# Splitting the first experts' weights on VectorE alone, in a routed encoder block in f32

## The chip, the cores and the metric

The kernel runs on one core of one Trainium2 chip. Its time is the device time of one execution in microseconds (us). Several runs were made; the median and the spread stand below, and one more execution was recorded by the hardware profiler.

## What is computed

One encoder block over 1024 positions of width 1024, in f32. A mixing half comes first (a Fourier group and windowed attention, an output projection, a gated residual). Then a mixture of 16 experts in which each expert chooses its 128 tokens:

```python
def expert_choice_moe(h, w_router, w_gate, w_up, w_down):
    cap = CAPACITY_FACTOR * S // N_EXPERTS          # 2 * 1024 / 16 = 128
    aff = jax.nn.softmax(h @ w_router, axis=-1)     # (S, 16)
    g, idx = lax.top_k(aff.T, cap)                  # each expert's 128 best tokens
    xin = h[idx]
    a, u = xin @ w_gate, xin @ w_up                 # 1024 x 1024 each, per expert
    y = (silu(a) * u) @ w_down * g
    return zeros.at[idx].add(y)
```

Each expert has three weight matrices of 4 MiB, 192 MiB for all sixteen. The change concerns only the second half, and its start above all.

## The kernel before

**Products in three parts.** A product of f32 values is made from three TensorE passes: both operands are split into a high part (the value rounded to TensorE's f32 format) and a low part (what is left), and hi x hi, lo x hi and hi x lo are summed (`mm3`, L71 to L74). `split` (L76 to L78) makes the parts: ScalarE copies the value into the high part (L77), then VectorE, or GpSimd where the caller says so, subtracts (L78). So in the profile L77 is a ScalarE piece of a split, and L78 the subtraction, on whichever engine it runs. `raw` is the tile that a load lands in, `wh` and `wl` are a weight unit's high and low part, `t0h`, `t0l`, `t1h`, `t1l` those of an expert's transposed tokens.

**Units and steps.** The expert weights are cut into 192 units of 1 MiB (256 rows by 1024 columns), four to a matrix, in the order gate 0, up 0, gate 1, down 0, up 1, gate 2, down 1, and so on (L962 to L967). A step is one unit's product, twelve matmuls of 512 columns. `load` (L970) issues a unit's load on SP's queue into one of 13 raw buffers; unit 13 goes into the buffer of unit 0, unit 14 into that of unit 1, so each can be loaded only once the other has been split. `cut_unit` (L989) splits the next unit into one of four pairs of `wh` and `wl`, and asks for the next load. `ahead` (L1140) keeps three units split ahead of the step that is about to run. In the kernel before, units 0 and 1 are split by GpSimd in four pieces each, as soon as they are loaded, while the last sort of the mixing half still runs; of units 6 to 23 the even ones go to GpSimd in two pieces, the odd ones to VectorE whole; all others go to VectorE.

**How the first experts are chosen.** While the last tile of the mixing half (t = 7) is projected, VectorE sorts the affinities of the tiles 0 to 5: steps of elementwise maximum and minimum over 32 x 64 elements (L805 and L806, tiles `sc` and `R`), and the result goes into `best` and `bestT`. L716 and L717 are the residual of the last tile, in two halves; L752 and L763 transpose it and form its affinities. From its affinities `choose` (L1063) finds the tokens of one expert in steps that wait for each other through TensorE; it runs for expert 0, then for expert 1. For the other 14 experts `thresholds` (L1106) sorts once more and counts; its steps are drawn in `product` between the first two experts' products, and its end is `dg` (L1115), a small product with it, a comparison (L1058, L1059), a count on TensorE (L1045, L1047) and `cn` (L1050).

**Gathering.** `gather_a` (L1161) makes eight marks for an expert (`oneh`, L1165: one where a position equals a slot), one per tile, on GpSimd or VectorE. `gather` (L1168) multiplies them with token numbers and gates on TensorE (L1173), VectorE forms the index `idx` (L1175), and GpSimd issues an indirect DMA that fetches the expert's rows from `h2d` into `xe` (L1182). `h2d` is in DRAM; the last tile's rows are written there at L1132. `flip` (L1186) transposes the tokens (L1192) and splits them. In the kernel before GpSimd makes two of the marks of expert 0 and four of those of expert 1, none of experts 2 and 3, and all of the later ones.

**Order.** Every engine works through its instructions in the order of the program. Where the code calls `in_order`, that order is the order in which the code was written, for the engines named; elsewhere a scheduler interleaves. The stretch from the second `choose` to the first product is pinned for TensorE, VectorE and GpSimd among its own instructions, and the experts' loop for all engines; the first instructions of the former can still be moved ahead of older ones. SP's queue is one line of loads and writes: a load that waits for a buffer holds up everything written behind it. The load of unit 11 (`HELD`) is held until the first gather has been issued.

Of the kernel before, what the change touches and what calls it, by code (L numbers as in the profile page):

```python
# [21 lines left out]
NT = 8  # L22
# [14 lines left out]
NSW, RATE0, RATE1, RATE2 = 5, 3.0, 2.0, 1.3  # L37
TK = 3

EARLY, LATER, HELD = (0, 1, 2, 3, 9, 10), (13, 14, 4, 5, 6, 7, 8), 11  # L40


@with_exitstack
def block_kernel(ctx: ExitStack, tc: tile.TileContext, t_in, out):
    nc = tc.nc
    PE, ACT, DVE, POOL, SP = nc.tensor, nc.scalar, nc.vector, nc.gpsimd, nc.sync
# [17 lines left out]
    def pt(name="pt"):  # L64
        return ps.tile([128, 512], F32, name=name, tag="pt", bufs=2)
# [10 lines left out]
    def split(hi, lo, src, eng=None):  # L76
        ACT.activation(hi, src, AF.Copy)  # L77
        return (eng or DVE).tensor_tensor(lo, src, hi.bitcast(F32), op=OP.subtract)  # L78
# [36 lines left out]
    def traced():  # L115
        return len(nc.cur_bb.bb.instructions)
# [10 lines left out]
    def drain(g):  # L127
        for _ in g:
            pass
# [836 lines left out]
    units_ = [(w[e], u) for w, e in groups for u in range(4)]  # L966
    NR = RAW1 + RAW2 + RAW3  # L967
    raws, cut = {}, []

    def load(m=None):  # L970
        if m is None:
            m = next((i for i in range(len(units_)) if i not in raws), None)
            if m is None:
                return
        src, u = units_[m]
        rp = raw3 if m % NR < RAW3 else raw2 if m % NR < RAW3 + RAW2 else raw1
        r = rp.tile([128, 2, D], F32, name="raw", tag="raw")
        if m == HELD:
            with tc.issue_after(after["p"].ins):
                POOL.memset(r[0:1, 0, 0:1], 0.0)  # L980
        v = src.rearrange("(k p) c -> p k c", p=128)[:, 2 * u:2 * u + 2, :]
        if m == len(units_) - 1:
            for k in range(2):
                SP.dma_start(r[:, k], v[:, k])
        else:
            SP.dma_start(r, v)
        raws[m] = r

    def cut_unit(eng=None, parts=1):  # L989
        m = len(cut)  # L990
        if m == len(units_):
            return
        r = raws[m]
        wp = wa if m % 4 in (0, 1) else wk
        h = wp.tile([128, 2, D], F32R, name="wh", bufs=2)
        l = wp.tile([128, 2, D], F32R, name="wl", bufs=2)
        for c in range(0, 2 * D, 2 * D // parts):
            hv, lv, rv = (o.rearrange("p k c -> p (k c)")[:, c:c + 2 * D // parts] for o in (h, l, r))
            split(hv, lv, rv, eng)
        cut.append((h, l))  # L1000
        if m > 1:
            load()

    pa, = banks(ctx, "psM", pa=6)
    for m in EARLY:
        load(m)
    for _ in range(2):
        cut_unit(POOL, 4)
    g2_r = wk.tile([128, D], F32, name="g2_r")
    tri = rt.tile([128, 128], BF, name="tri")  # L1010
    r1 = rt.tile([128, NT, NE], F32, name="r1")
# [29 lines left out]
    def counted(gq, es):  # L1041
        m = gq.shape[1]
        n = gq.shape[2]
        p = pa()
        PE.matmul(p[:, :m * n], tri, gq.rearrange("p a e -> p (a e)"), start=True, stop=False)  # L1045
        for a in range(m - 1):
            PE.matmul(p[:, (a + 1) * n:m * n].rearrange("p (a e) -> p a e", e=n), ones_b,  # L1047
                      gq[:, a:a + 1, :].to_broadcast([128, m - 1 - a, n]), start=False, stop=(a == m - 2))
        c = rt.tile([128, m, n], F32, name=f"cn{n}")
        DVE.scalar_tensor_tensor(c.rearrange("p a e -> p (a e)"), p[:, :m * n], 1.0, gq.rearrange("p a e -> p (a e)"),  # L1050
                                 op0=OP.add, op1=OP.mult)
        return c

    def at_least(th, nt, es):
        n = es.stop - es.start
        gq = rt.tile([128, 2 * nt, n], BF, name=f"gq{n}")
        th = th[:, None, :].to_broadcast([128, nt, n])
        DVE.tensor_tensor(gq[:, :nt], aff[:, :nt, es], th, op=OP.is_gt)  # L1058
        DVE.tensor_tensor(gq[:, nt:], aff[:, :nt, es], th, op=OP.is_equal)  # L1059
        return gq  # L1060


    def choose(e):  # L1063
        p = pt()
        for i in range(2):
            PE.matmul(p[:, i * 128:i * 128 + 128], aff[:, OLD + i, e:e + 1].to_broadcast([128, 128]), ident,
                      start=True, stop=True)
        acc = rt.tile([128, 5], F32, name="acc")
        v6, v7 = aff[:, OLD, e:e + 1], aff[:, OLD + 1, e:e + 1]

        def above(a, val):
            junk = rt.tile([128, 256], BF, name="junk", bufs=2)
            return DVE.scalar_tensor_tensor(junk, p[:, :256], val, ones, op0=OP.is_gt, op1=OP.mult, accum_out=acc[:, a:a + 1])

        above(0, best[:, e:e + 1])
        kept = rt.tile([128, 1], BF, name="kept")
        k0 = DVE.tensor_scalar(kept, acc[:, 0:1], rank0, 127.0, op0=OP.add, op1=OP.is_le)
        with tc.issue_after(k0.ins):
            above(1, v6)
        yield  # L1080
        pn = pa()
        PE.matmul(pn[:, :1], ones_b, kept, start=True, stop=True)
        edge = rt.tile([128, 1], F32, name="edge")
        e0 = DVE.scalar_tensor_tensor(edge, pn[:, :1], rank1, best[:, e:e + 1], op0=OP.is_equal, op1=OP.mult)
        with tc.issue_after(e0.ins):
            above(3, v7)
            for a, val, w, wid in ((2, v6, below, 128), (4, v7, both, 256)):
                junk = rt.tile([128, 256], BF, name="junk", bufs=2)
                DVE.scalar_tensor_tensor(junk[:, :wid], p[:, :wid], val, w, op0=OP.is_equal, op1=OP.mult,
                                         accum_out=acc[:, a:a + 1])  # L1090
        yield
        pe = pa()
        PE.matmul(pe[:, :1], ones[:, 0:128], edge, start=True, stop=True)
        gq = at_least(pe[:, :1], OLD, slice(e, e + 1))
        yield
        c = counted(gq, slice(e, e + 1))
        a, b = c[:, :OLD, 0], c[:, OLD:, 0]
        DVE.tensor_tensor(a, a, b, op=OP.add)
        DVE.scalar_tensor_tensor(pos[:, :OLD, e], a, pn[:, :1], a, op0=OP.is_le, op1=OP.mult)
        for i in range(2):  # L1100
            r = acc[:, 1 + 2 * i:2 + 2 * i]
            DVE.scalar_tensor_tensor(r, r, 1.0, acc[:, 2 + 2 * i:3 + 2 * i], op0=OP.add, op1=OP.add)
            DVE.tensor_tensor(pos[:, OLD + i, e:e + 1], r, pn[:, :1], op=OP.add)
# [36 lines left out]
    def ahead(la):  # L1140
        while len(cut) <= step[0] + la and len(cut) < len(units_):
            m = len(cut)
            if 6 <= m < 24 and m % 2 == 0:
                cut_unit(POOL, 2)
            else:
                cut_unit(None, 2 if m == len(units_) - 1 else 1)

    def product(acc, xh, xl, la=3, halves=False):
        n = step[0]
        u = n % 4  # L1150
        if n:
            drain(itertools.islice(rest, 3))
        ahead(la)
        step[0] += 1
        wh, wl = cut[n]
        for k, hf in ((0, 0), (1, 0), (0, 1), (1, 1)) if halves else ((0, 0), (0, 1), (1, 0), (1, 1)):
            kc = 2 * u + k
            cs_ = slice(hf * 512, hf * 512 + 512)
            mm3(acc[hf], xh[:, kc, :], xl[:, kc, :], wh[:, k, cs_], wl[:, k, cs_], kc == 0, kc == 7)

    def gather_a(e):  # L1161
        shared = (2, 4, 0, 0)[e] if e < 4 else NT
        oneh = wk.tile([128, NT, 128], BF, name="oneh", bufs=1)
        for t in range(NT):
            (POOL if t < shared else DVE).tensor_scalar(oneh[:, t, :], slots, pos[:, t, e:e + 1], None, op0=OP.is_equal)  # L1165
        return oneh
# [19 lines left out]
    def flip(src, e):  # L1186
        h = wk.tile([128, 8, 128], F32R, name=f"t{e % 2}h", bufs=1)
        l = wk.tile([128, 8, 128], F32R, name=f"t{e % 2}l", bufs=1)
        for b in range(2):
            p = pt()  # L1190
            for k in range(4):
                PE.transpose(p[:, k * 128:k * 128 + 128], src[:, (4 * b + k) * 128:(4 * b + k + 1) * 128], ident)  # L1192
            split(h[:, 4 * b:4 * b + 4], l[:, 4 * b:4 * b + 4], p.rearrange("p (a b) -> p a b", b=128))
        return h, l
# [18 lines left out]
    gs = {}  # L1213
    gather(0)
    tp = traced()
    while len(raws) < NR + 2:
        load()
    SP.dma_start(g2_r, md[3:4, :].to_broadcast([128, D]))
    c1 = choose(1)
    next(c1)  # L1220
    next(c1)
    cut_unit(parts=2)
    drain(c1)
    oneh = gather_a(1)
    xh, xl = flip(gs[0][2], 0)
    cut_unit()

    def selection():
# [117 lines left out]
```

## Time and profile before

| | us |
|---|---|
| median of 3 runs | 1079.47 (1076.07 to 1079.58) |
| the profiled execution | 1078.71 |
| its span in the profile | 1076.9 |
| PE busy | 969.0 (90%) |
| DVE busy | 845.9 (79%) |
| ACT busy | 636.9 (59%) |
| POOL busy | 540.3 (50%) |
| chain that ended last, by engine | PE 64%, DVE 15%, issue 6%, ACT 4%, DMA 2%, POOL 2% |

PE is TensorE, PEld its weight loads, DVE VectorE, ACT ScalarE, POOL GpSimd, SP the engine that issues most DMAs. A row of a timeline has the start in us from the span's start, the duration in us, the engine, the line, the operation, the tile written and those read, the shapes and a count; in brackets stand the engine's idle time before it and what ended that. A row of a stage has its length, the busy time of each engine with its number of instructions, the clock granted to TensorE (1.00 is full), the share of time that the 16 DMA engines were busy, and GB/s. A row of waits has who waited for whom, the sum in us, how often, and the longest. The later experts fill the span from about 558 us on; the routing of the first ones lies between about 400 and 558 us.

### The profile page before, as it was taken

What the parts mean: (1) busy time and instruction counts of PE and PEld (TensorE: products, weight loads), DVE (VectorE), ACT (ScalarE), POOL (GpSimd) and SP (SyncE); (2) the same over time, 40 slices, a digit from 0 to 9 for tenths busy, and PEclk for the clock granted to TensorE, in tenths of its full rate; (3) what the DMA queues carried; (4) which work ended last, traced back from release to release, by engine and by line L of the source; (5) the groups of instructions that cost most, each with busy time, mean ns of one, the idle gap of its engine ahead of it and who ended that gap; (6) DMA issues with size and microseconds to landing.
All of it is one profiled execution on the core that took longest, in us unless ns stands there. A gap on an engine that the chain in (4) does not pass through costs nothing.

```text
span 1076.9 us, 13229 instructions
## 1 busy us (share of the span) xinstructions
PE 969.0 (90%) x4681; PEld 756.4 (70%) x4681; DVE 845.9 (79%) x1223; ACT 636.9 (59%) x846; POOL 540.3 (50%) x345
## 2 busy tenths in 40 slices
PE   4797999979999996496769999999999999999996
PEld 3675767747777675374658777877787778777885
DVE  6845884687666959689688898889888988898894
ACT  3353434576455442264437777777777777777782
POOL 2646465132433334355472875587558755772203
PEclk9798999979999999598889999999999999999998
DMA  9765674262312136895689999999999999999922
GB/s 318 246 210 212 220 266 150 82 195 61 111 70 89 65 132 215 326 321 192 229 260 339 410 372 374 369 411 370 373 369 411 371 371 371 411 371 358 376 110 40
DMA packets 95499, 283.97 MB, mean 264 GB/s; under 512 B 7892, under 2 KB 25480, under 8 KB 95304
## 3 DMA queue, kind: packets, MB, share of 16 engines
q1 hardware_dynamic: 90824, 266.34, 66.7%
q0 software_dynamic: 4608, 16.78, 6.1%
q8 instruction: 37, 0.61, 0.2%
q14 instruction: 30, 0.25, 0.1%
HBM read 263.79 MB, written 21.40 MB: 265 GB/s over the span
## 4 chain that ended last, share of the span: by engine, by line
PE 64%; DVE 15%; issue 6%; ACT 4%; DMA 2%; POOL 2%; POOLq 0%; DVEq 0%; ACTq 0%; SPq 0%
PE pa L72 13%; PE pa L73 13%; PE pa L74 13%; PE pu L332 4%; PE pt L1192 2%; ACT wh L77 2%; PE pt L640 2%; PE yp L653 2%; DVE sc L805 2%; DVE wl L78 2%; PE pj L74 2%; PE pj L72 2%; PE pj L73 2%; DVE sc L806 2%; DVE ws L113 2%
## 5 line engine op out<-in xcount | busy, mean ns | idle before, releaser
L78 DVE TENSOR_TENSOR wl<-raw,wh 128x2048 fp32r<-128x2048 f32 (+1 forms) x183 | 418.1, 2309 | 63.5 <-ACT wh L77 62.6
L77 ACT ACTIVATE wh<-raw 128x2048 fp32r<-128x2048 f32 (+2 forms) x209 | 367.8, 1780 | 85.0 <-PE pa L73 81.3
L1165 POOL TENSOR_SCALAR oneh<-tri_f,pos 128x128 bf16<-128x128 f32 x102 | 189.5, 1871 | 4.1 <-PE pa L1047 3.3
L73 PE MATMUL pa<-wh,t1l 128*128 128x512 f32 x384 | 151.8, 395 | 7.8 <-DVE t1l L78 7.8
L72 PE MATMUL pa<-wh,t0h 128*128 128x512 f32 x384 | 155.8, 406 | 0.0
L73 PE MATMUL pa<-wh,t0l 128*128 128x512 f32 x384 | 153.4, 400 | 0.0
L72 PE MATMUL pa<-wh,t1h 128*128 128x512 f32 x384 | 153.1, 399 | 0.0
L74 PE MATMUL pa<-wl,t0h 128*128 128x512 f32 x384 | 152.6, 397 | 0.0
L74 PE MATMUL pa<-wl,t1h 128*128 128x512 f32 x384 | 151.3, 394 | 0.0
L1207 POOL TENSOR_TENSOR ys<-ys,g_r 128x512 f32<-128x512 f32 x30 | 53.5, 1803 | 124.7 <-ACT ys L1206 124.7
L73 PEld LDWEIGHTS pa<-wh,t1l 128*128 128x128 f32 x384 | 72.6, 189 | 24.0 <-DVE t1l L78 8.3
L74 PEld LDWEIGHTS pa<-wl,t0h 128*128 128x128 f32 x384 | 73.6, 192 | 17.0
L72 PEld LDWEIGHTS pa<-wh,t0h 128*128 128x128 f32 x384 | 73.6, 192 | 16.2 <-ACT t0h L77 0.2
L73 PEld LDWEIGHTS pa<-wh,t0l 128*128 128x128 f32 x384 | 73.6, 192 | 16.1 <-DVE t0l L78 0.4
L74 PEld LDWEIGHTS pa<-wl,t1h 128*128 128x128 f32 x384 | 72.6, 189 | 17.0 <-DVE wl L78 0.4
L72 PEld LDWEIGHTS pa<-wh,t1h 128*128 128x128 f32 x384 | 72.4, 189 | 15.9
L1182 POOL DMA_INDIRECT xe<-h2d,idx x16 | 16.9, 1055 | 115.7 <-DVE gt L1179 110.7
L78 POOL TENSOR_TENSOR wl<-raw,wh 128x1024 fp32r<-128x1024 f32 (+1 forms) x26 | 56.7, 2208 | 22.3 <-ACT wh L77 22.2
L78 POOL TENSOR_TENSOR hl<-hf,hh 128x512 fp32r<-128x512 f32 (+1 forms) x20 | 25.5, 1274 | 62.9 <-ACT hh L77 43.6
L1210 POOL DMA_INDIRECT out_dram<-ys,idx x16 | 50.9, 3183 | 10.6 <-DVE ys L1209 6.4
L611 DVE CUSTOM_DVE_ANT_0 sb<-lg,bias,sink 128x384 f32<-128x384 f32 (+1 forms) x64 | 35.0, 579 | 26.7 <-PE lg L609 15.7
L233 ACT ACTIVATE hf<-pt,sh1c,G1c 128x128 f32<-128x128 f32 (+1 forms) x56 | 22.6, 479 | 53.3 <-PE pt L226 36.2
(310 smaller groups left out, 1809.5 us busy)
## 6 DMA issues: line engine op xcount, KB each, us to landing
raw<-in_w_gate_dram SPq DMA_DIRECT2D x64, 1024.0 KB
raw<-in_w_up_dram SPq DMA_DIRECT2D x64, 1024.0 KB
raw<-in_w_down_dram SPq DMA_DIRECT2D x63, 1024.0 KB
raw<-in_w_ada_dram SPq DMA_DIRECT2D x16, 1024.0 KB
raw<-in_w_ada_dram SPq DMA_DIRECT2D x16, 512.0 KB
xt<-in_x_dram SPq DMA_DIRECT2D x8, 512.0 KB
raw<-in_w_out_dram SPq DMA_DIRECT2D x4, 1024.0 KB
raw<-in_x_dram SPq DMA_DIRECT2D x8, 512.0 KB
```

The costliest lines, as they stand in the source:

```text
L72: PE.matmul(o, lh, rh, start=start, stop=False)
L73: PE.matmul(o, ll, rh, start=False, stop=False)
L74: return PE.matmul(o, lh, rl, start=False, stop=stop)
L77: ACT.activation(hi, src, AF.Copy)
L78: return (eng or DVE).tensor_tensor(lo, src, hi.bitcast(F32), op=OP.subtract)
L113: DVE.scalar_tensor_tensor(acc, u[:, j, :], w, acc, op0=OP.mult, op1=OP.add)
L233: ACT.activation(hf[:, a * w:a * w + w], tp[:, a * w:a * w + w], AF.Identity, scale=G1c[:, kc:kc + 1], bias=sh1c[:, kc:kc + 1])
L332: PE.matmul(acc[:, :c1 - c0], lhs, r[kc][:, c0:c1], start=(kc == 0 and l == 0 and r is w_h), stop=(kc == 7 and r is w_l))
L611: DVE.tensor_tensor_reduce(sb[:, :wid], lg[:, :wid], bias[:, kv * 4 + i, j0:j0 + wid], 1.0, sk[:, i:i + 1], op0=OP.add, op1=OP.max, accum_ ...
L1165: (POOL if t < shared else DVE).tensor_scalar(oneh[:, t, :], slots, pos[:, t, e:e + 1], None, op0=OP.is_equal)
L1207: POOL.tensor_tensor(ys[:, cs_], ys[:, cs_], g2_r[:, cs_], op=OP.mult)
L1210: POOL.indirect_dma_start(out=out2, out_offset=bass.IndirectOffsetOnAxis(ap=idx[:, :1], axis=0), in_=ys, in_offset=None, compute_op=OP.add)
```

## The change

Three things are changed. GpSimd splits no expert weights any more: `cut_unit` loses its engine argument, and `ahead` the rule for units 6 to 23. Units 0 and 1 are no longer split at the start of the stage, but later, in two pieces each: unit 0 behind the first gather, unit 1 between the second and the third step of `choose(1)`; units 2 and 3, whole, behind the first flip. Because `load` of units 13 and 14 needs the buffers of units 0 and 1, they are taken out of `LATER`, and every `cut_unit` now asks for a load. And the marks of experts 0 to 3 are all made by VectorE.

```diff
-EARLY, LATER, HELD = (0, 1, 2, 3, 9, 10), (13, 14, 4, 5, 6, 7, 8), 11
+EARLY, LATER, HELD = (0, 1, 2, 3, 9, 10), (4, 5, 6, 7, 8), 11
...
-    def cut_unit(eng=None, parts=1):
+    def cut_unit(parts=1):
...
-            split(hv, lv, rv, eng)
+            split(hv, lv, rv)
         cut.append((h, l))
-        if m > 1:
-            load()
+        load()
...
     for m in EARLY:
         load(m)
-    for _ in range(2):
-        cut_unit(POOL, 4)
...
     def ahead(la):
         while len(cut) <= step[0] + la and len(cut) < len(units_):
             m = len(cut)
-            if 6 <= m < 24 and m % 2 == 0:
-                cut_unit(POOL, 2)
-            else:
-                cut_unit(None, 2 if m == len(units_) - 1 else 1)
+            cut_unit(2 if m == len(units_) - 1 else 1)
...
     def gather_a(e):
-        shared = (2, 4, 0, 0)[e] if e < 4 else NT
+        shared = 0 if e < 4 else NT
...
     gs = {}
     gather(0)
     tp = traced()
-    while len(raws) < NR + 2:
+    while len(raws) < NR:
         load()
     SP.dma_start(g2_r, md[3:4, :].to_broadcast([128, D]))
+    cut_unit(2)
     c1 = choose(1)
     next(c1)
     next(c1)
-    cut_unit(parts=2)
+    cut_unit(2)
     drain(c1)
     oneh = gather_a(1)
     xh, xl = flip(gs[0][2], 0)
+    cut_unit()
     cut_unit()
```

In the rows of the changed kernel below, lines up to L986 are numbered as before; from L1010 on to `ahead` they read three lower (L1016 is L1013), behind it six (L1165 is L1159).

VectorE, at the end of the last sort. Before, from its last merge steps to the second half of the last tile's residual (`raw<-lg,g_r`, then `raw<-raw`):

```order
L806 TENSOR_TENSOR sc<-sc 32x16x4
L805 TENSOR_TENSOR sc<-sc 32x32x2
L806 TENSOR_TENSOR sc<-sc 32x32x2
L805 TENSOR_TENSOR R<-sc 32x64
L806 TENSOR_TENSOR R<-sc 32x64
L857 STREAM_TRANSPOSE best<-R 32x32 x4
L858 COPY bestT<-R 16x128
L1014 CAST tri<-r_4143 128x128
L1033 TENSOR_TENSOR r_4143<-aff,aux 128x96
L716 TENSOR_TENSOR raw<-lg,g_r 128x512
```

And now, from the first half of unit 0's split:

```order
L78 TENSOR_TENSOR wl<-raw,wh 128x1024
L805 TENSOR_TENSOR sc<-sc 32x2x32
L806 TENSOR_TENSOR sc<-sc 32x2x32
L805 TENSOR_TENSOR sc<-sc 32x4x16
L806 TENSOR_TENSOR sc<-sc 32x4x16
L78 TENSOR_TENSOR wl<-raw,wh 128x1024
L805 TENSOR_TENSOR sc<-sc 32x8x8
L806 TENSOR_TENSOR sc<-sc 32x8x8
L1011 CAST tri<-r_4123 128x128
L805 TENSOR_TENSOR sc<-sc 32x16x4
L806 TENSOR_TENSOR sc<-sc 32x16x4
L716 TENSOR_TENSOR raw<-lg,g_r 128x512
```

Unit 0's two halves have come in between the steps, ahead of where the code has them, and the residual has moved from behind the sort and the copies of its result to ahead of its last two pairs of steps.

SP, from the weights that are loaded last before the first gather to the write of the last tile's rows (`h2d`), the difference of the two orders:

```order
-L1022 DMA tok<-in_k_tok_dram 128x16
-L986 DMA raw<-in_w_down_dram 128x2x1024 x2
+L1010 DMA r_4123<-in_k_tri_dram 128x128
+L1013 DMA tri_f<-in_k_tri_dram 128x3x128
+L1019 DMA tok<-in_k_tok_dram 128x16
 L986 DMA raw<-in_w_up_dram 128x2x1024 x4
 L986 DMA raw<-in_w_gate_dram 128x2x1024
-L1132 DMA h2d<-raw 128x1024
-L1133 DMA out_dram<-raw 128x1024
+L1129 DMA h2d<-raw 128x1024
+L1130 DMA out_dram<-raw 128x1024
```

The two loads of `w_down`, units 13 and 14, are gone from ahead of the write; they now stand behind the load of `g_r`, after the first gather.

VectorE, at the end of `thresholds`, among the products of the second expert's turn. Before:

```order
L1115 TENSOR_SCALAR dg<-ident,R 16x16
L78 TENSOR_TENSOR wl<-raw,wh 128x2048
L1058 TENSOR_TENSOR gq_4745<-aff,pt 128x120
L1059 TENSOR_TENSOR gq_4745<-aff,pt 128x120
L1050 SCALAR_TENSOR_TENSOR cn_4785<-pa,gq_4745 128x240
L1125 TENSOR_TENSOR pos<-cn_4785 128x8x15
L1165 TENSOR_SCALAR oneh<-tri_f,pos 128x128 x8
```

And now:

```order
L1112 TENSOR_SCALAR dg<-ident,R 16x16
L78 TENSOR_TENSOR wl<-raw,wh 128x2048
L1055 TENSOR_TENSOR gq_4725<-aff,pt 128x120
L1056 TENSOR_TENSOR gq_4725<-aff,pt 128x120
L78 TENSOR_TENSOR wl<-raw,wh 128x2048
L1047 SCALAR_TENSOR_TENSOR cn_4763<-pa,gq_4725 128x240
L1122 TENSOR_TENSOR pos<-cn_4763 128x8x15
L1159 TENSOR_SCALAR oneh<-tri_f,pos 128x128 x8
```

A second unit's split, which GpSimd had, stands between the comparison and `cn`. In the same way one more split stands on VectorE at every second step of the first two experts.

## The prediction

> **What bounds the kernel now.** I read the chain that ended last in order of time, then the busy time by stage, then who TensorE waited for, then VectorE's and GpSimd's own timelines where it waited. The chain, from the end of routing:
>
> ```profile
> 441.33 8.78 DMA h2d<-raw
> 451.02 5.22 DMA xe<-h2d,idx
> 456.28 1.97 PE pt L1192 x8
> ...
> 558.26 0.87 PE pt L1192 x8
> ...
> 588.25 1.93 ACT wh L77
> ...
> 624.11 1.92 ACT wh L77
> ```
>
> The first gather waits for the last tile's write to h2d. From 558 us on the same row returns every 35.86 us, one expert. The stages (PE, PEld, DVE, ACT, POOL busy, clock, DMA share, GB/s):
>
> ```profile
> 459.00:558.00 99.00, 73.15 (x318) 57.56 (x319) 85.11 (x127) 46.28 (x42) 58.24 (x28) 0.83 0.73 254
> 566.00:1030.00 464.00, 460.15 (x2171) 371.27 (x2170) 403.81 (x282) 349.70 (x260) 281.92 (x139) 1.00 1.01 379
> ```
>
> Later experts are TensorE's: 460.15 of 464 us. In the first stage TensorE has 73 of 99 us, VectorE 85. TensorE's waits from 456 to 600 us:
>
> ```profile
> PE pt L1119 <- DVE dg L1115: 9.5, 1, 9.5
> PE pt L1173 <- DVE oneh L1165: 8.5, 3, 4.3
> PE pa L73 <- DVE t1l L78: 7.8, 1, 7.8
> ```
>
> All three name VectorE: 25.8 us. And VectorE is held up. The short sort steps beside GpSimd's splits (start, duration):
>
> ```profile
> 417.19 1.35 POOL L78 TENSOR_TENSOR wl<-raw,wh 128x512 fp32r<-128x512 f32 x1 [1.33 <-ACT wh L77]
> 417.29 1.32 DVE L805 TENSOR_TENSOR sc<-sc 32x64 f32<-32x64 f32 x1
> ...
> 421.69 0.21 DVE L806 TENSOR_TENSOR sc<-sc 32x64 f32<-32x64 f32 x1
> 421.71 8.69 POOL L78 TENSOR_TENSOR wl<-raw,wh 128x512 fp32r<-128x512 f32 x7 [3.17 <-ACT wh L77]
> 421.94 1.21 DVE L805 TENSOR_TENSOR sc<-sc 32x64 f32<-32x64 f32 x1
> 423.07 1.30 DVE L806 TENSOR_TENSOR sc<-sc 32x64 f32<-32x64 f32 x1
> ...
> 430.41 0.20 DVE L806 TENSOR_TENSOR R<-sc 32x64 f32<-32x64 f32 x1
> ```
>
> A step takes 0.21 us until GpSimd's split starts, then 1.2 to 1.3, which is one GpSimd piece (8.69 / 7 = 1.24), and 0.20 again once GpSimd is done. I read that as exclusion: one step slips in after each piece.
>
> **The change: before the first product.** Removed: the eight quarter splits of units 0 and 1 on GpSimd. Seven steps took 430.41 - 421.94 = 8.5 us; at 0.21 they take 1.5. With the one at 417.29 (1.32 to 0.21) that is 7.0 + 1.1 = 8.1 us back. Added: unit 0's two halves, which the order puts between those steps; a pair cost 2.36 us, below. Moved: the last tile's second half (L716, L717) used to stand behind the sort, and now stands before its last pairs.
>
> ```profile
> 419.54 0.67 DVE L717 TENSOR_TENSOR raw<-raw 128x512 f32<-128x512 f32 x1
> ...
> 432.09 0.69 DVE L716 TENSOR_TENSOR raw<-lg,g_r 128x512 f32<-128x512 f32 x1
> ...
> 447.35 0.22 DVE L1175 TENSOR_SCALAR idx<-pt 128x1 int32<-128x1 f32 x1
> ...
> 449.43 2.36 DVE L78 TENSOR_TENSOR wl<-raw,wh 128x1024 fp32r<-128x1024 f32 x2
> ...
> 453.55 0.90 DVE L1165 TENSOR_SCALAR oneh<-tri_f,pos 128x128 bf16<-128x128 f32 x4
> 458.06 0.69 DVE L78 TENSOR_TENSOR t0l<-pt,t0h 128x512 fp32r<-128x512 f32 x1 [3.62 <-ACT t0h L77]
> ```
>
> New start of L716: L717's end (420.2) less 1.1; plus a shuffle, a merge and three pairs, which took until 421.9, 1.7; two more pairs 0.8; the halves 2.4; a cast, taken as a step, 0.2: 424.2. So what follows from that half comes 7.9 us earlier; the index, with two more marks on VectorE (0.4), at 447.35 - 7.5 = 439.9.
>
> The write to h2d is then issued at 441.33 - 7.9 = 433.4. With its 8.78 us it lands at 442.2. But ahead of it SP used to have seven loads, and now has five:
>
> ```profile
> 423.32 0.40 PE L74 MATMUL lg<-wol,yah 128*128 128x512 f32 x1
> ...
> 425.55 5.26 SPq L986 DMA_DIRECT2D raw<-in_w_down_dram  x2
> 430.90 2.16 SPq L986 DMA_DIRECT2D raw<-in_w_up_dram  x4
> 433.10 0.49 SPq L986 DMA_DIRECT2D raw<-in_w_gate_dram  x1
> ...
> GB/s 318 246 210 212 220 266 150 82 195 61 111 70 89 65 132 215 326 321 192 229 260 339 410 372 374 369 411 370 373 369 411 371 371 371 411 371 358 376 110 40
> ```
>
> The two of w_down (units 13 and 14) waited for GpSimd, and the others behind them on SP. At 411 GB/s, the highest rate of the slices, 1 MiB is 2.55 us, two are 5.1. Five loads from about 423 us, when the last output product (first row) ends, take 12.8 and are through near 437 with a start of about 1 us; the write's half MiB takes 1.3 and lands near 440, together with the index. Bounds: 7.9 us (queue as long as before) to 10.4 (the index alone); I take 10, since the two loads are gone for certain. VectorE must then be ready for the flip at 458.06 - 10 = 448.1: its last marks end at 454.45 - 7.5 + 0.8 (four more marks) = 447.8. This covers the added work with 0.3 us to spare; any more lies on the path. Unit 2's split moves behind the flip (2.28 us); two products (35.86 / 12 = 3 us each) cover it.
>
> **The stage of the first experts.** VectorE's groups between 459 and 558 us, GpSimd's splits, VectorE's sort (tile sc), and marks without GpSimd beside them:
>
> ```profile
> L78 DVE TENSOR_TENSOR wl<-raw,wh 128x2048 fp32r<-128x2048 f32 x12 | 31.1, 2596 | 4.1 <-ACT wh L77 4.1
> L1165 DVE TENSOR_SCALAR oneh<-tri_f,pos 128x128 bf16<-128x128 f32 x16 | 9.5, 670 | 0.0
> ...
> L78 POOL TENSOR_TENSOR wl<-raw,wh 128x1024 fp32r<-128x1024 f32 x18 | 46.7, 2618 | 17.8 <-ACT wh L77 17.7
> ...
> 459.00:558.00 99.00, 31.68 (x46) 0.83 0.73 254
> ...
> 525.88 1.67 DVE L1165 TENSOR_SCALAR oneh<-tri_f,pos 128x128 bf16<-128x128 f32 x8
> 527.46 2.29 DVE L78 TENSOR_TENSOR wl<-raw,wh 128x2048 fp32r<-128x2048 f32 x1
> ```
>
> Before: 31.1 + 9.5 + 31.7 and 12.8 of other work make 85.1. After, with nothing of GpSimd's splits beside it: 12 units, the 9 from GpSimd and unit 2 are 22 x 2.28 = 50.2; sort 46 x 0.21 = 9.7; marks 16 x 0.21 = 3.3; other 12.8: 76.0 us. So ten units cost 22.8 us more, and 31.9 us of being held go away.
>
> VectorE's idle time in the stage is 99 - 85.1 = 13.9 us. Most of it, with 559 us taken in:
>
> ```profile
> DVE cn L1050 <- PE pa L1047: 4.4, 1, 4.4
> DVE wl L78 <- ACT wh L77: 4.1, 1, 4.1
> DVE t1l L78 <- ACT t1h L77: 3.3, 1, 3.3
> DVE idx L1175 <- PE pt L1173: 1.9, 2, 1.6
> ```
>
> The order now puts another unit's split ahead of cn (2.3 of the 4.4) and unit 3's ahead of idx (1.6): at most 10.0 us stay, at least none. I take 7, near the upper end, because ScalarE's ys and hs still stand ahead of the next wh. The stage: 76 + 7 = 83 for 99, a gain of 16 (13 to 23). TensorE needs 73 us or less for it, so VectorE sets its end. The waits of 25.8 us shrink, not vanish.
>
> **The sum.** The profiled execution is 1078.71 us (span 1076.9), 0.8 under the median. 1078.7 - 10 - 16 = **1053 us**; by the bounds 1058 to 1045. The later experts are TensorE's and move as a whole.
>
> **Does DMA let them?** Its share is 1.01 from 566 to 1030, and the two loads now come later. SP's own waits from 560 to 1040 us:
>
> ```profile
> SPq L986 <- DVE wl L78: 354.6, 142, 7.4
> ```
>
> SP waits most of the time for a free buffer, not for the queue, so TensorE's pace sets the loads. An expert's 12 loads take 12 x 2.55 = 30.6 us of its 35.86. The Trainium skill speaks against this in SBUF — State Buffer, Summary: rules for kernel authors: it has transfers from HBM reckoned at about 358 GB/s; an estimate by it is 2.93 us a load and 35.2 an expert without the gathers, so DMA would be the pace and nothing would be gained. The row above, 379 GB/s over 464 us, is over that rate, and the trace decides.
>
> **Rivals.** *DMA is the pace* of the later experts: the end stays, or comes later by the two loads' 5.1 us: 1079 to 1084. For: share 1.01. Against: SP's waits, and 0.73 in the stage to catch up in. *The front stays*: something else keeps the first gather (the write's queue, or VectorE late with the added splits); only 16 us: 1063. For: the cover of 0.3 us. *The idle time grows* with VectorE as the only splitter: the stage gives 7 instead of 16: 1062. For: ScalarE and TensorE are in one loop with VectorE through four weight buffers. *The other side*: the stretch is not GpSimd's doing, and the short steps stay long because of something that remains. Then VectorE gets 22.8 us more in the stage and 2.4 in the sort: 1078.7 + 25 = 1104. It decides once less than 25 of the 8.1 + 31.9 us come back. Against: at 421.71 and 430.41 the stretch begins and ends with GpSimd's run. That the change is not made as told is excluded by the order.
>
> **How the numbers follow.** Forecast (1045 to 1058): 0.71. Front stays: 0.09. Idle grows: 0.08. Better than 1045: 0.04. DMA the pace: 0.04. Other side: 0.04. A measurement here tells about 0.5% (5.4 us) from no change: faster 0.71 + 0.09 + 0.08 + 0.04 = 0.92, same 0.04, slower 0.04. The range takes in the two smaller gains: 1044 to 1066.
>
> **What would show it.** Right: no sort step over 0.7 us after 417 us; the write to h2d issued near 433.4, the gather near 441, the transposes of 558.26 near 532; VectorE busy some 76 of 83 us there, TensorE's waits about half; every expert after that 35.86 us. Wrong: sort steps of over a microsecond with GpSimd idle; a first product no earlier than 455; TensorE waiting for wh with ScalarE waiting for raw (DMA); VectorE idle over 14 us in the stage.

## The result and the profile after

The changed kernel takes 1045.9 us (median of 4 runs, 1044.96 to 1046.96), the kernel before beside it 1078.91 us. The ratio is 0.9693, 95% interval 0.9675 to 0.9712: 33 us faster, where 26 were forecast. The profiled execution took 1045.42 us, with a span of 1043.6 us, 33.3 under that of before.

The two stages of the profile after, in the columns of the prediction's stage rows: from the first flip's low part to the transposes that stood at 558.26 us before, and a stretch of later experts as long as the one shown of before:

```profile
445.44:524.45 79.01, 70.45 (x320) 55.35 (x321) 73.99 (x139) 45.65 (x33) 12.69 (x9) 0.92 0.93 341
532.00:996.00 464.00, 460.15 (x2171) 371.21 (x2170) 403.60 (x282) 349.57 (x260) 283.97 (x139) 1.00 1.01 379
```

Before, the first of these ran from 458.06 to 558.26 us, 100.2 us; now it takes 79.0, and it starts 12.6 us earlier. VectorE is busy for 74.0 of the 79.0 us, TensorE's clock has gone from 0.83 to 0.92. The second row has TensorE's busy time, 460.15 us, and the 379 GB/s of before to the last digit: the later experts run as they did.

The routing before the first product, on VectorE, SP and GpSimd (start, duration), from the sort steps beside unit 0's halves to the first flip:

```profile
419.15 0.21 DVE L806 TENSOR_TENSOR sc<-sc 32x64 f32<-32x64 f32 x1
419.28 1.21 DVE L78 TENSOR_TENSOR wl<-raw,wh 128x1024 fp32r<-128x1024 f32 x1
420.42 0.20 DVE L805 TENSOR_TENSOR sc<-sc 32x64 f32<-32x64 f32 x1
...
422.89 0.67 DVE L716 TENSOR_TENSOR raw<-lg,g_r 128x512 f32<-128x512 f32 x1
...
437.68 0.22 DVE L1169 TENSOR_SCALAR idx<-pt 128x1 int32<-128x1 f32 x1
...
443.88 1.65 DVE L1159 TENSOR_SCALAR oneh<-tri_f,pos 128x128 bf16<-128x128 f32 x8
445.44 1.28 DVE L78 TENSOR_TENSOR t0l<-pt,t0h 128x512 fp32r<-128x512 f32 x2
```

```profile
416.91 0.61 SPq L1019 DMA_DIRECT2D tok<-in_k_tok_dram  x1
417.62 4.37 SPq L986 DMA_DIRECT2D raw<-in_w_up_dram  x4
422.03 0.74 SPq L986 DMA_DIRECT2D raw<-in_w_gate_dram  x1
432.32 0.34 SPq L1129 DMA_DIRECT2D h2d<-raw  x1
```

```profile
438.20 1.20 POOL L1176 DMA_INDIRECT xe<-h2d,idx  x1 [5.91 <-DVE gt L1173]
```

The sort steps take 0.2 us with a split on either side of them. The residual has come from 432.09 to 422.89 us, the index from 447.35 to 437.68, and the gather now follows the index within 0.52 us, where it used to come 3.67 us after it and waited for the write. The five loads no longer wait; SP issues them right behind the token table.

VectorE's groups in the stage of the first experts (busy, mean ns of one), the time of its sort (tile `sc`) there up to the third expert's `hs`, and what VectorE waited for:

```profile
L78 DVE TENSOR_TENSOR wl<-raw,wh 128x2048 fp32r<-128x2048 f32 x22 | 50.3, 2298 | 1.8 <-ACT wh L77 1.8
L1159 DVE TENSOR_SCALAR oneh<-tri_f,pos 128x128 bf16<-128x128 f32 x16 | 3.3, 278 | 0.0
```

```profile
445.44:559.21 113.77, 8.12 (x46) 0.94 0.92 334
```

```profile
DVE wl L78 <- ACT wh L77: 1.8, 1, 1.8
DVE idx L1169 <- PE pt L1167: 0.7, 2, 0.4
```

The 46 sort instructions took 31.68 us and take 8.12, the marks 9.5 and now 3.3; 22 splits take 50.3. TensorE's waits, from 430 to 600 us:

```profile
PE pt L1167 <- DVE oneh L1159: 4.6, 2, 3.6
...
PE pt L1186 <- DVE hs L1268: 2.5, 3, 1.9
...
PE pt L1116 <- DVE dg L1112: 1.4, 1, 1.4
...
PE pa L73 <- DVE t1l L78: 0.9, 1, 0.9
...
PE pa L73 <- DVE t0l L78: 0.8, 1, 0.8
```

The three waits of 25.8 us are now 4.6 + 1.4 + 0.9 = 6.9 (1.0 of them lies ahead of the first flip, outside the stretch that the prediction counted); those for `hs` have grown from 0.3 to 2.5, and one of 0.8 for `t0l` is new. The prediction had the three at half; they are about a quarter.

### The profile page after: what moved, and what is told of

Same layout as the page of the kernel before. It is cut to its first block, busy times and chain, and to the rows that moved or that the text cites. A ratio compares the mean times of both kernels' runs of the same rounds, so it can differ in the third digit from the quotient of the medians.

```text
span 1043.6 us, 13198 instructions
## 1 busy us (share of the span) xinstructions
PE 964.2 (92%) x4681; PEld 752.6 (72%) x4681; DVE 828.4 (79%) x1241; ACT 636.1 (61%) x832; POOL 482.6 (46%) x313
## 4 chain that ended last, share of the span: by engine, by line
PE 64%; DVE 14%; issue 7%; ACT 4%; POOL 3%; DMA 1%; POOLq 0%; SPq 0%; DVEq 0%; ACTq 0%
PE pa L73 13%; PE pa L72 13%; PE pa L74 13%; PE pu L332 4%; DVE wl L78 3%; PE pt L1186 2%; ACT wh L77 2%; PE pt L640 2%; PE yp L653 2%; PE pj L74 2%; PE pj L72 2%; PE pj L73 2%; DVE ws L113 2%; PE lg L608 1%; PE pt L763 1%
## 5 line engine op out<-in xcount | busy, mean ns | idle before, releaser
L78 DVE TENSOR_TENSOR wl<-raw,wh 128x2048 fp32r<-128x2048 f32 (+1 forms) x195 | 439.6, 2278 | 61.4 <-ACT wh L77 60.7
L77 ACT ACTIVATE wh<-raw 128x2048 fp32r<-128x2048 f32 (+1 forms) x195 | 366.5, 1893 | 77.8 <-PE pa L73 74.7
L1159 POOL TENSOR_SCALAR oneh<-tri_f,pos 128x128 bf16<-128x128 f32 x96 | 187.8, 1969 | 0.5
L113 DVE SCALAR_TENSOR_TENSOR ws<-raw,c_act,ws 128x512 f32<-128x512 f32 x56 | 49.0, 875 | 1.1
```

Of the source, the lines that this page charges most:

```text
L113: DVE.scalar_tensor_tensor(acc, u[:, j, :], w, acc, op0=OP.mult, op1=OP.add)
```

## The experiments

**The theory.** GpSimd's splits hold VectorE's work, since the two engines exclude each other while both have operands to fetch; in front the first gather starts at the later of two things, the index (held by the stretched sort) and the landing of the write (held by the loads ahead of it). Rivals: what before lost lay in handing work over through waits and buffers; or in where the first two units are split, whoever does it; or the three edits' costs simply add.

The span drifts by up to 5 us between executions before the routing begins, so the traces are compared from one instruction that is alike in all of them, the start of L731 on the residual of tile 6, the last tile but one (412.05 us in before, 411.39 in after). The columns: from there to the index, to the first gather, to the first flip's low part (`t0l`); from `t0l` to the first `hs` product (L1268) of the third expert; from there to the end. All in us.

| kernel | index | gather | `t0l` | to the third `hs` | rest |
|---|---|---|---|---|---|
| before | 35.30 | 38.97 | 46.01 | 134.95 | 483.9 |
| after | 26.29 | 26.81 | 34.05 | 113.77 | 484.4 |
| after, once more | 26.30 | 26.82 | 34.07 | 115.35 | 483.8 |
| even units on GpSimd again | 26.30 | 26.82 | 34.06 | 136.44 | 484.1 |
| early on GpSimd, loads ahead | 34.65 | 38.91 | 45.39 | 114.97 | 484.2 |
| early on GpSimd, no loads ahead | 34.63 | 35.15 | 42.40 | 114.94 | 484.1 |
| early on VectorE, loads ahead | 27.67 | 35.89 | 42.29 | 114.24 | 484.3 |
| early on VectorE, no loads ahead | 27.93 | 28.45 | 35.71 | 114.98 | 483.9 |
| marks on GpSimd again | 26.95 | 27.47 | 33.97 | 113.76 | 484.2 |
| idle subtractions on GpSimd | 26.29 | 26.81 | 34.06 | 136.83 | 484.4 |
| idle fills on GpSimd | 26.29 | 26.81 | 34.06 | 117.66 | 484.2 |
| last addition on VectorE | 24.32 | 24.84 | 32.08 | 116.53 | 484.5 |
| last addition on VectorE, once more | 24.84 | 25.35 | 32.60 | 116.67 | 484.2 |

From before to after: 0.66 us of drift, 12.0 in front, 21.2 in the first experts, 0.5 lost behind: 33.3. The experiments change the front and the first experts apart from each other, and the last column never moves by more than 0.7.

**The even units alone.** Units 6 to 22, even, go back to GpSimd; the rest is the changed kernel.

```diff
...
-            cut_unit(2 if m == len(units_) - 1 else 1)
+            if 6 <= m < 24 and m % 2 == 0:
+                cut_unit(2, POOL)
+            else:
+                cut_unit(2 if m == len(units_) - 1 else 1)
```

> The changed kernel, with the even units 6 to 22 split by GpSimd again, in two pieces each; all else as changed. Theory (exclusion: a subtraction on GpSimd and a VectorE operation that reads two tensors from SBUF never run together): the routing before the first product stays as changed (gather near 438 us), and in the stage of the first experts sort steps and marks take over a microsecond again, though VectorE has nine splits fewer: 1066 us (1062 to 1071). Rival (the units were late because GpSimd is slow, 4.7 us a unit, and nothing is held up): the sort steps stay at 0.21 us, TensorE waits for wl of GpSimd, 1055 to 1060. Rival (the gain came from the queue and the order before the first product alone): 1046.

Measured: 1067.54 us, ratio to before 0.9884 (0.9862 to 0.9906), 21.6 us over the changed kernel. The stage and the time of its sort:

```profile
448.98:551.08 102.10, 75.57 (x324) 59.24 (x325) 88.14 (x130) 46.33 (x42) 58.82 (x29) 0.80 0.74 271
```

```profile
448.98:551.08 102.10, 31.85 (x46) 0.80 0.74 271
```

Nine units out of VectorE's hands leave it busier, 88.1 us: the same 46 sort instructions are back at 31.85 us. The front keeps its whole gain. So the splits of the even units on GpSimd are worth 21 to 22 us by themselves. A sort step beside one of GpSimd's pieces, which here have 128 x 1024 elements, and the first one after them (GpSimd's row ends at 479.31 us):

```profile
467.76 11.55 POOL L78 TENSOR_TENSOR wl<-raw,wh 128x1024 fp32r<-128x1024 f32 x4 [0.49 <-ACT wh L77]
```

```profile
477.02 2.36 DVE L806 TENSOR_TENSOR sc<-sc 32x64 f32<-32x64 f32 x1
479.42 0.21 DVE L805 TENSOR_TENSOR sc<-sc 32x64 f32<-32x64 f32 x1
```

Beside the pieces of half that size in the sort of before a step took 1.2 to 1.3 us: the length of a held step goes with the length of GpSimd's piece, as exclusion has it.

**The first two units early on GpSimd, with and without two loads ahead.** The first kernel restores the place (and, through the scheduler, the order in which the residual stands behind the sort) and the loads of units 13 and 14 ahead of the write; the second leaves out the line that orders those loads.

```diff
-EARLY, LATER, HELD = (0, 1, 2, 3, 9, 10), (4, 5, 6, 7, 8), 11
+EARLY, LATER, HELD = (0, 1, 2, 3, 9, 10), (13, 14, 4, 5, 6, 7, 8), 11
...
+    for _ in range(2):
+        cut_unit(4, POOL)
...
-    cut_unit(2)
     c1 = choose(1)
...
-    cut_unit()
```

> The changed kernel, with units 0 and 1 split early by GpSimd in four pieces each, and units 13 and 14 loaded ahead of the write of the last tile's rows, as before the change. Theory (exclusion, in the last sort): the stage of the first experts stays at 79 us, the gather goes back to about 451 us: 1058 (1055 to 1061). Rival (what held up VectorE before the first product is small against the stage): 1046 to 1050.

> As the run with units 0 and 1 early on GpSimd, but units 13 and 14 are not loaded ahead of the write of the last tile's rows. Theory (the sort held up by GpSimd is what delays the index; the two loads add a delay of their own only to the write): the sort steps take 1.2 us again, the index is there at about 447 and the gather starts right then: 1055 (1053 to 1057), some 3 us under the run with the loads. Rival (the two loads ahead of the write are the cause): the gather starts near 438, 1046 to 1048.

Measured: 1057.25 us (ratio 0.9797, 0.9781 to 0.9813) and 1053.88 us (0.9766, 0.975 to 0.9783). VectorE and GpSimd in the first:

```profile
421.92 0.21 DVE L806 TENSOR_TENSOR sc<-sc 32x64 f32<-32x64 f32 x1
422.16 1.21 DVE L805 TENSOR_TENSOR sc<-sc 32x64 f32<-32x64 f32 x1
423.30 1.31 DVE L806 TENSOR_TENSOR sc<-sc 32x64 f32<-32x64 f32 x1
...
446.93 0.22 DVE L1172 TENSOR_SCALAR idx<-pt 128x1 int32<-128x1 f32 x1
```

```profile
451.19 1.23 POOL L1179 DMA_INDIRECT xe<-h2d,idx  x1 [9.66 <-DMA h2d<-raw]
```

And GpSimd in the second, whose index was at 445.33 us:

```profile
445.85 1.20 POOL L1179 DMA_INDIRECT xe<-h2d,idx  x1 [5.91 <-DVE gt L1176]
```

In the first the gather stands 4.26 us behind the index and waits for the write; in the second it stands 0.52 us behind, at an index as late. So with a late index the loads cost 3.8 us in the trace, 3.4 in the medians.

**The same place, but split by VectorE.** Two more kernels, the same with `cut_unit(4)` in place of `cut_unit(4, POOL)`: GpSimd splits nothing, the units stay early.

> The changed kernel with the place of the first two units put back (split early, each in four pieces; units 13 and 14 loaded ahead of the last tile's write), but by VectorE, so that GpSimd splits nothing. It tells who splits apart from where the splits stand. Theory (what cost the time was GpSimd's pieces holding VectorE's sort steps): no sort step over 0.7 us after 417 us except beside the one GpSimd addition that is left at 413 us, and 1049 us (1046 to 1052): the changed kernel's 1045.9 plus at most the 3.4 us by which the run without the two loads ahead beat the run with them, and some pieces of VectorE's own between the steps. Rival (the early place itself, and the order of the second choice that goes with it, cost the time, whoever splits): 1057, as in the run with the early place on GpSimd.

> The first two units split early by VectorE, as in the run that took 1053.42, but units 13 and 14 are not loaded ahead of the last tile's write. This fills the fourth corner: who splits early (GpSimd or VectorE) against two loads ahead or none. Theory (the first gather starts at the later of two things, the index and the landing of the write; GpSimd's pieces set the one, the loads ahead the other, so either cure alone gives 3 to 4 us and both give the whole): the gather right behind an index near 437.5, 1046 (1044.5 to 1047.5), 7 to 8 us under the run with the loads ahead. Rival (the two costs add): 1050, that is 1053.4 less the 3.4 us which the loads cost in the pair of runs with GpSimd.

Measured: 1053.42 us (0.978, 0.9744 to 0.9816) with the loads ahead, 1047.40 us (0.9706, 0.9674 to 0.9738) without. The first is above its 1046 to 1052. VectorE and SP in it, then the chain around its first gather (start, us):

```profile
422.00 0.21 DVE L806 TENSOR_TENSOR sc<-sc 32x64 f32<-32x64 f32 x1
422.13 0.67 DVE L716 TENSOR_TENSOR raw<-lg,g_r 128x512 f32<-128x512 f32 x1
...
437.54 0.22 DVE L1172 TENSOR_SCALAR idx<-pt 128x1 int32<-128x1 f32 x1
```

```profile
426.72 0.37 SPq L986 DMA_DIRECT2D raw<-in_w_down_dram  x1
427.19 1.65 SPq L986 DMA_DIRECT2D raw<-in_w_up_dram  x3
428.88 0.47 SPq L986 DMA_DIRECT2D raw<-in_w_gate_dram  x1
432.02 0.34 SPq L1132 DMA_DIRECT2D h2d<-raw  x1
```

```profile
432.02 12.82 DMA h2d<-raw
...
445.76 4.57 DMA xe<-h2d,idx
```

The sort steps are short again and the index stands at 437.54 us, 27.67 us after L731, for 26.29 in the changed kernel. But the write, issued at 432.02 us behind loads of 5 MiB that were issued from 426.72 on, takes 12.82 us, and the gather comes 8.2 us after the index. The stretch from the write's issue to its landing (columns of a stage) shows the DMA engines busy all the time:

```profile
432.00:444.80 12.80, 4.02 (x42) 3.22 (x41) 11.84 (x66) 0.34 (x1) 0.00 (x0) 0.50 0.98 376
```

Without the two loads ahead, the index was at 440.33 us and the gather followed at once:

```profile
440.85 1.20 POOL L1179 DMA_INDIRECT xe<-h2d,idx  x1 [6.06 <-DVE gt L1176]
```

So the rival that the place itself costs the time is out: early and by VectorE the front is within 1.7 us of the changed kernel's. And the two costs do not add. From L731 to the gather, the loads' removal alone gives 3.8 us, VectorE's splitting alone 3.0, both 10.5. Each cure alone uncovers the other's limit; it is a maximum of two, index and landing. VectorE's part holds two things, the stretch and the residual's place in the order, which the scheduler chose with it; no run separates them. An estimate from the two traces without loads ahead: the second half of the residual (L716) starts 20.04 us after L731 with GpSimd's splits and 12.26 with VectorE's, and in the former 1.7 us lie between the last sort step and the residual (429.05 to 430.74 us), so most of the 7.8 us is the stretch.

**The marks alone.** The two and four marks of experts 0 and 1 go back to GpSimd (`shared = (2, 4, 0, 0)[e] if e < 4 else NT`).

> The changed kernel, with two marks of expert 0 and four of expert 1 made by GpSimd as before. Theory: 0.7 us of GpSimd for a mark against 0.2 of VectorE, and both hold each other up, so nothing is won: 1046 (1045 to 1048). Rival (the marks on VectorE stand on the path to the first product, 1.3 us): 1044.5.

Measured: 1045.76 us (0.9691, 0.9675 to 0.9707). The index comes 0.66 us later than in the changed kernel, `t0l` 0.08 earlier, since the way from the gather to `t0l` takes 6.50 us for 7.24: the two effects cancel, and this edit is worth nothing here.

**GpSimd busy with nothing.** The changed kernel with work on GpSimd that no one waits for, at the nine places where before split on it: four subtractions, or twelve fills, of 128 x 512 each (`spare` is a tile that nobody reads, `o2` a constant of ones).

```diff
+            if 6 <= m < 24 and m % 2 == 0:
+                for _ in range(4):
+                    POOL.tensor_tensor(spare.rearrange("p (a b) -> p a b", a=2), o2, o2, op=OP.subtract)
```

```diff
+            if 6 <= m < 24 and m % 2 == 0:
+                for _ in range(12):
+                    POOL.memset(spare, 0.0)
```

> The changed kernel with work added on GpSimd whose result nobody reads: 36 subtractions of 128 x 512 elements, four at each of the nine even units 6 to 22, where before split these units on GpSimd. VectorE still splits everything; no DMA and no buffer is touched by them. Theory (GpSimd's two-input pieces hold VectorE's two-input steps, one slipping in per piece): some 36 x 1.2 = 43 us of GpSimd's time lie in the stage of the first experts against VectorE, which is busy for 74 of its 79 us; the stage grows by 20 to 40 us and the kernel takes 1065 to 1086. Rival (GpSimd's pieces hold nothing; what before lost was the hand-over of the splits through buffers and waits): 1046 (1044.5 to 1047.5).

> As the run with idle subtractions, but with idle fills: 108 of 128 x 512 elements on GpSimd, which only write and read nothing, twelve at each of the nine even units. Theory (it is two-input work on GpSimd that excludes VectorE's): 1046 (1044.5 to 1049), the stage of the first experts within 2 us of the changed kernel's 78.9. Rival (any work on GpSimd holds VectorE): as with the subtractions, 1065 or more.

Measured: 1070.0 us (0.9916, 0.9891 to 0.9941) with the subtractions, inside the theory's 1065 to 1086, and 1049.65 us (0.9724, 0.9701 to 0.9747) with the fills, just above the upper end of what was expected. First the subtractions: the splits and the sort steps of VectorE up to the third expert's `hs`, then all of its sort there:

```profile
L78 DVE TENSOR_TENSOR wl<-raw,wh 128x2048 fp32r<-128x2048 f32 x33 | 80.5, 2453 | 7.3 <-ACT wh L77 7.2
L805 DVE TENSOR_TENSOR sc<-sc 32x64 f32<-32x64 f32 x12 | 11.8, 987 | 0.3
...
L806 DVE TENSOR_TENSOR sc<-sc 32x64 f32<-32x64 f32 x12 | 2.5, 206 | 0.0
```

```profile
445.74:582.57 136.83, 19.45 (x46) 0.87 0.79 278
```

The same with the fills:

```profile
L78 DVE TENSOR_TENSOR wl<-raw,wh 128x2048 fp32r<-128x2048 f32 x33 | 77.9, 2376 | 7.1 <-ACT wh L77 7.1
...
L805 DVE TENSOR_TENSOR sc<-sc 32x64 f32<-32x64 f32 x12 | 2.5, 211 | 0.3
```

```profile
444.46:562.12 117.66, 8.12 (x46) 0.93 0.90 322
```

The first experts as a whole, in the changed kernel, with the subtractions and with the fills (columns of a stage; VectorE is the third, GpSimd the fifth):

```profile
445.44:559.21 113.77, 105.21 (x485) 83.76 (x486) 101.94 (x158) 72.69 (x53) 23.08 (x18) 0.94 0.92 334
```

```profile
445.74:582.57 136.83, 111.35 (x485) 87.51 (x486) 122.86 (x158) 72.69 (x53) 94.33 (x54) 0.87 0.79 278
```

```profile
444.46:562.12 117.66, 106.17 (x486) 84.38 (x486) 105.43 (x159) 72.72 (x53) 89.73 (x126) 0.93 0.90 322
```

And what the fills held up on GpSimd itself:

```profile
518.32 14.63 POOL L1145 MEMSET spare<- 128x512 f32 x24
533.15 1.58 POOL L1181 DMA_INDIRECT xe<-h2d,idx  x1 [0.20 <-issue]
```

VectorE's program is the same in both, and GpSimd is busy about as long, 94 and 90 us. Work on GpSimd that hands over nothing makes the first experts 23 us longer if it reads (136.83 for 113.77), with twelve of the short steps at 987 ns on average in place of 211; if it only writes, the sort is unmoved at 8.12 us. Of the 23.1 us, 20.9 are VectorE's own instructions taking longer (122.86 busy for 101.94), 11.3 of them in the sort. This is the case for exclusion, and against the hand-over of splits as the cause. The Trainium skill has this rule in SBUF — State Buffer, Who interferes with whom: a VectorE instruction with two inputs from SBUF contends with a GpSimd instruction that reads SBUF, not with one that only writes it. The two `sc` rows agree, 19.45 against 8.12 us. Two things do not fit so neatly. Beside the subtractions only every other short step is long (L806 keeps its 206 ns), so one held step for every step is not the rule there, and that the total comes so near the 136.44 us of the even units' splits, whose sort took 31.85, is chance. And the fills are not free: the first experts took 117.66 us, for 113.77 and 115.35 of the changed kernel. The fourth expert's gather, whose index was ready at 521.09 us, was issued at 533.15, behind the fills, but TensorE did not wait for its rows. VectorE was busy 3.5 us longer (105.43 for 101.94); what held it there is not shown.

**The last long step.** In the changed kernel one sort step still takes 2.05 us, at 413.22 us beside GpSimd's addition L732 of tile 6 (2.44 us from 412.75). Here VectorE makes that addition.

```diff
-            POOL.tensor_tensor(h2[:, c], h2[:, c], sh2_r[:, c], op=OP.add)
+            (DVE if t == 6 else POOL).tensor_tensor(h2[:, c], h2[:, c], sh2_r[:, c], op=OP.add)
```

> The changed kernel with the last long sort step taken away as well: the addition of tile 6 (L732), beside which one sort step still takes 2.05 us at 413 us, is made by VectorE. Theory (each such piece of GpSimd costs the step beside it, less what VectorE pays for doing the work): 1045.2 (1044.4 to 1046.0), 0.7 us gained at the most. Rival (this place is off the path, or VectorE's own 0.7 us for the addition stands in the step's place): 1045.9.

Measured: 1044.64 us (0.9679, 0.9655 to 0.9703). The trace had the gather 2.0 us earlier, but the first experts 1.2 to 2.8 us longer. So it was run again on one chip beside the changed kernel:

> The changed kernel, unaltered, beside the kernel with the last addition on VectorE on the same chip: 1045.9 (1044.9 to 1047.0).

> The kernel with the addition of tile 6 on VectorE again, beside the changed kernel on the same chip. If its 1.3 us were real: 1044.6, with the changed kernel at 1045.9. If the later start of the third expert that its trace showed is the rule: both within 0.5 us of each other.

Measured: 1045.33 us for the changed kernel (0.9699, 0.9671 to 0.9726), 1044.88 us for the other (0.9686, 0.9661 to 0.971). The intervals cover each other; no gain is shown, though the front's 1.5 to 2.0 us were there in both traces. No version beat the changed kernel by more than the measurement can tell.

## Why the prediction was right, point by point

- **The total.** 1045.9 us lies 0.9 above the fast end of the forecast's 1045 to 1058. The mechanism was right, both terms were too small, and the front's 12.0 us is outside its own bounds of 7.9 to 10.4; that the sum stayed inside is luck to this extent, since the stage's 21.2 kept 1.8 under its bound of 23.
- **Exclusion.** Right, and shown: the even units alone give 21.6 us, and idle subtractions take them away again (24.1). The other side (1104 us) would have needed the short steps to stay long without GpSimd's splits; they fell to 0.2 us.
- **The residual at 424.2 us.** It came at 422.89: 0.66 of that is drift, 0.6 an overstated stretch of shuffle, pairs and halves.
- **The index at 439.9.** It came at 437.68. Besides the residual's 1.3 us, the term for two more marks on VectorE had the wrong sign: the prediction added 0.4, the run with the marks back on GpSimd has the index 0.66 us *later*.
- **The write.** This step failed. "Five loads from about 423 us, when the last output product ends" set the landing near 440. Their buffers were free and SP issued them from 417.62 us, right behind the token table; what had held them was the two loads of units 13 and 14 alone. So the write set no bound, the gather came at 438.20 for the predicted 441, and the front gave 12.0 us (12.6 with the drift) for 10. Where loads did hold the write, early by VectorE with the two ahead, the same reckoning (five loads of 2.55 us from 426.7, about 1 us of start, 1.3 for the write) gives 441.8 us; it landed at 444.84, at 376 GB/s and not 411. No row shows the start of about 1 us, and the prediction's own terms add up to 438.3 us, not to 440.
- **The cover of 0.3 us.** It was not there. ScalarE's first high part of the tokens was ready at 444.51 us, and VectorE, at its last marks until 445.53, began the low part at 445.44; TensorE waited 0.8 us for `t0l`, as the waits above show. The way from gather to `t0l` has still grown by only 0.2 us (7.24 for 7.04), because the gathered rows came 0.7 us sooner (4.55 us from the gather's start to the transposes, for 5.26).

```profile
443.91 0.60 ACT L77 ACTIVATE t0h<-pt 128x512 fp32r<-128x512 f32 x1 [10.49 <-PE pt L1186]
```

- **The stage at 83 us.** 79.0. VectorE's work is 74.0 us for 76: the splits (50.3) and marks (3.3) are as worked out, the sort is 8.1 for 9.7, since the 0.21 us was taken for every one of the 46, and successive steps overlap. Idle time is 5.0 for 7: of the 4.4 and 1.9 us before `cn` and `idx` only 0.7 stayed. And the 99 us of before was a round window, 1.2 us shorter than the stage itself. Together the stage gave 21.2 for 16, 5 of the 7 us by which the gain was undersized.
- **DMA as the pace** did not come: the later experts run at 379 GB/s and 460.15 busy us of TensorE as before, and the last column of the table is unchanged. By the rule of 358 GB/s (the Trainium skill, SBUF — State Buffer, Summary: rules for kernel authors) nothing would have been gained; the trace decides against it.
- **The rivals that the front stays or the idle time grows** did not come either. The first was nearer than it looked: with the units split early by VectorE and the loads still ahead, the front gave 3 us and the kernel stood at 1053.

## What to carry to other kernels

Before giving an idle engine some of a busy engine's elementwise work, compare the busy engine's short instructions with and without the helper beside them: here nine units taken off VectorE cost it more in stretched sort steps (31.85 for 8.12 us, 23.7) than splitting them itself (9 x 2.28, 20.5). Where a start waits for the later of two things, price each cure with the other in place: alone they gave 3.8 and 3.0 us, together 10.5. A load that waits for a buffer delays every transfer written behind it in its queue, so look for what stands in front of a small write that someone waits for.

## What was not expected of the hardware

Half a MiB written to DRAM at 432.02 us, with 5 MiB of loads issued in the 5.3 us ahead of it, took 12.82 us, in which the DMA engines moved 4.8 MB (376 GB/s), most of it those loads. The same write in the changed kernel, at 432.32 us behind five loads that SP had issued by 422.8, was done within 5.9 us. The same program's first three experts took 113.77 and 115.35 us in two traces, so differences of 1 to 2 us there are read from several runs or not at all.
